# A scheduler's model learns the VectorE-GpSimd lock, and the low parts of the weights go to VectorE alone

## The chip, the cores and the metric

The kernel runs on one core of a Trainium2 chip. A core has a matrix engine (TensorE, PE in the profile, with PEld for the loading of its stationary operand), a vector engine (VectorE, DVE), an activation engine (ScalarE, ACT), a programmable engine (GpSimd, POOL) and a sync engine that here issues all DMAs (SyncE, SP). Each engine takes its own instructions strictly in order and waits on semaphores for the others. The metric is the device time of one execution in microseconds; lower is better.

## The reference

Two layers over 256 latent tokens and 256 context tokens of 1024 features. Layer 0 mixes tokens with a bidirectional RG-LRU, layer 1 with a bidirectional gated DeltaNet; each is followed by a SwiGLU feed-forward block (FFN), and each sub-layer is normalised and modulated by vectors that come from `c` and `c_ctx`. Cut to what matters:

```python
for layer in range(2):
    mod_l = split(silu(c) @ ada_w[layer] + ada_b[layer], 6)       # mod_c from c_ctx alike
    h = modulate(rmsnorm(x, norm_g[layer, 0]), mod_l[0], mod_l[1])
    if layer == 0:   # RG-LRU: u, y = split(h @ w_in); conv over 4 tokens; gates = sigmoid(u @ gate_w)
        a = exp(8 * r_gate * log_sigmoid(lam)); b = sqrt(1 - a * a) * (i_gate * u)
        y = (linear_scan(a, b) + reverse_scan(a, b)) * gelu(y) @ w_out
    else:            # gated DeltaNet: 8 key heads, 16 value heads of 128
        q, k, v = silu(conv(h @ w_in)); chunked: solve (I + strict(k k^T * decay)) u = rhs, state S
        y = (rmsnorm(o) * silu(z)) @ w_out
    x = x + mod_l[2] * y
    h = modulate(rmsnorm(x, norm_g[layer, 1]), mod_l[3], mod_l[4])
    x = x + mod_l[5] * ((silu(h @ w_gate) * (h @ w_up)) @ w_down)
return rmsnorm(x, final_norm_g)
```

## The kernel before

All products of weights run in a reduced-precision float32 format with both operands split in two parts: `hi` is the value rounded to that format, `lo = value - hi`. `mm3` adds three products (hi·hi, hi·lo, lo·hi). A weight tile of 128 x 1024 float32 comes by one DMA of 512 KB into `raw`; a copy with a change of type makes `whi`, and a subtraction makes `wlo` from `raw` and `whi`. Both happen in `weight()`, once for each of some 240 weight tiles; `split()` does the same for activations (`uh`/`ul`, `oh`/`ol`, `fh`/`fl`). So every weight tile costs one cast and one subtraction of 1024 columns on the element-wise engines before TensorE can use it.

The program is not written in the order in which it runs. A `Recorder` notes every instruction with its operands; at the end of a stage `flush()` gives them to a list scheduler. It keeps a clock for each engine, takes an estimate of each instruction's duration from `_cost()`, and places next the ready instruction with the lowest priority number (its place in the program plus a bias of its stage from the table `TUNE`). Some instructions have a choice of engine: `R.copy`, `R.scaled`, `R.plus` may go to ACT or DVE, `R.tt` (add, subtract or multiply of SBUF operands) to DVE or POOL; the scheduler takes the engine that by its estimates is done first. The order in the profile, L544 on every line, is what this left.

Before the change, `weight()` put `wlo` on DVE or POOL by `R.tt` in the stages marked wide (RG-LRU, both FFNs, output product) and in the z gates, and always on POOL in the rest of DeltaNet and for the weights that are made ahead of a stage (`aside=True`).

The stages in order of time, with the names that appear below:

- start: loads, norm, modulation of the first sub-layer (`ps_ada`)
- RG-LRU: products `ps_mm`, gate products `ps_g` from `uh`, `ul`; gates and scans (`th`, `nv`, `iu`, `a`) in 128 x 512 tiles on DVE; output `oh`, `ol`
- FFN of layer 0: gate and up products (`sg`, `fh`, `fl`), then down (`ps_dn`). Beside it the six modulation vectors of layer 1 are summed in the spare half of `x2` (the profile's `x<-ring,cs,x`, `x<-x,ring`)
- norm and modulation of layer 1 (`xg`, `hh`, `hl`, the last through `h` for half of the tiles)
- DeltaNet, in the order that `PROG` names by letters: A (products of a key head, convolution `cu` on DVE), E (decays `gn`, loaded by DMA from `rows`, masked by an affine select on POOL), N (systems of two key heads; elimination inside 32 x 32 blocks, one system to a lane: 30 steps of two dependent DVE instructions, `lmul<-lw` and `lw<-lw,lmul`), L (the blocks joined by small products on TensorE, `ps_w`, `ps_z`), P and C (attention weights `at`, queries `qg`, then the state over four chunks: `r`, `ps_y`, `S`, `kw`, `vb`), Z (z gates). There are four groups 0 to 3 of two key heads
- output product `ps_wo`, FFN of layer 1, final norm

Of the kernel before, what the change touches and what calls it, by code (L numbers as in the profile page):

```python
# [12 lines left out]
F32 = mybir.dt.float32  # L13
F32R = mybir.dt.float32r
AF = mybir.ActivationFunctionType
OP = mybir.AluOpType
# [10 lines left out]
# columns of the packed small-parameter array  # L27
# [10 lines left out]
# ---------------------------------------------------------------- program order  # L38
# The kernel is written down stage by stage; a list scheduler then orders the instructions of all
# engines, earlier stages first, so that later independent work fills an engine's waits. Tiles are  # L40
# allocated when their first instruction is placed.
def _shuffle(sh, pattern, sizes):
    """einops-like rearrange of a numpy array"""
# [33 lines left out]
class _Tile:  # L77
    def __init__(self, pool, shape, dtype, tag, bufs, name, dram):
# [7 lines left out]
        # a bank of PSUM is one region: its readers wait for all products into it  # L86
# [6 lines left out]
        self.group = [-1] * 4       # last product into the bank, per 32 partitions  # L93
        self.used = {}              # a bank serves one engine at a time: its last use by each
# [5 lines left out]
class _AP:  # L100
    """an access pattern of a tile that may not have its place yet"""
# [34 lines left out]
    def raw(self, offset, ap):  # L136
        """any pattern over a DRAM tile"""
        return self._with(("raw", offset, ap), self.sh)
# [25 lines left out]
class _Op:  # L164
    __slots__ = ("alts", "args", "kw", "tiles", "deps", "prio", "idx", "bytes", "succ", "ndep", "ready", "fin", "rows", "cols", "narrow")


_TABLE = {"Tanh": 7, "Exp": 1, "Gelu_apprx_tanh": 2, "Silu": 4, "Sqrt": 8}     # sets that hold the function
# [28 lines left out]
class Recorder:  # L197
    DMA_RATE = 360.0        # bytes / ns
    DMA_LATENCY = 2000
    TICK, TICK_COLUMNS = 10240 / 3, 3300  # L200
    # from the end of an instruction to the start of one that waits for it
# [15 lines left out]
    # ---- instructions with a choice of engine  # L217
# [22 lines left out]
    def tt(self, out, a, b, op):  # L240
        """add, subtract or mult of SBUF operands"""
# [3 lines left out]
    def mark(ap):  # L245
        """the instructions that have written ap so far, for after= of a later one"""
# [9 lines left out]
    # ---- costs in ns  # L256
    def _cost(self, eng, method, out, ins, kw, args):
        n = out.free() if isinstance(out, _AP) else 1
        src_psum = any(i.t.psum for i in ins) or (isinstance(out, _AP) and out.t.psum)
        if eng == "PE":  # L260
# [8 lines left out]
            if m <= 64:         # the column groups run side by side  # L269
# [3 lines left out]
        if eng == "DVE":  # L273
            if method == "transpose":
                return 1.04 * n + 70
# [12 lines left out]
        if eng == "POOL":  # L288
            if method == "dma_start":
                return 1000  # L290
            if method in ("memset", "affine_select"):
                return 0.6 * n + 60
            if kw.get("op", args[3] if len(args) > 3 else None) == OP.pow:
                return 165 * n + 298
            return 2.2 * n + 100
        return 60

# [255 lines left out]
def hybrid_block(ctx: ExitStack, tc: tile.TileContext, I, out, dbg=None):  # L553
# [1048 lines left out]
    X = {}  # L1602
# [117 lines left out]
```

## Time and profile before

| | us |
|---|---|
| three runs: median (lowest, highest) | 1481.32 (1480.1, 1487.81) |
| profiled execution: span from the first to the last instruction | 1474.6 |
| median less that span (what lies around it, and the spread of the runs) | 6.7 |
| busy in the profiled execution: PE / DVE / ACT / POOL | 1329.7 / 1149.3 / 552.4 / 430.8 |

The profiled execution has no time of its own beside its span. A busy time counts an instruction from its start to its end as the profile models it. PE's is no measure of its load, since matmuls overlap in the pipeline; its load is better read from the number of matmuls in a stretch. The last columns of a table by stretches are the granted TensorE clock (PEclk, 1.00 is full) and the DMA share. In a group of instructions the figures after the bar are busy us, mean ns of one, idle time of the engine before them, and what ended that idle time. A tile's view gives minimum, median and maximum in ns.

### The profile page before, as it was taken

To read this page: it belongs to the slowest core of one execution; us is meant where nothing else is said; L and a number is where in the kernel's file an instruction comes from. 1 tells how busy PE (TensorE), PEld (TensorE's weight loads), DVE (VectorE), ACT (ScalarE), POOL (GpSimd) and SP (SyncE) were. 2 spreads that over 40 slices of the span, in tenths; PEclk is the share of its full clock that TensorE was granted. 3 is DMA by queue.
4 is the path that set the end of the run, shared out by engine and by line. 5 is a ranking of instruction groups with operands and counts; after the bars stand their busy time and mean duration, and the time that the engine had idled before them with its cause. 6 is when DMAs were issued, how large, how long until landed. Compare 5 with 4: busy or idle time off the path is not lost.

```text
span 1474.6 us, 23548 instructions
## 1 busy us (share of the span) xinstructions
PE 1329.7 (90%) x9195; PEld 1135.7 (77%) x9195; DVE 1149.3 (78%) x1802; ACT 552.4 (37%) x1069; POOL 430.8 (29%) x357
## 2 busy tenths in 40 slices
PE   6998989999999999988767997888888898899997
PEld 3676758787778777886656786777788797899997
DVE  6899996778888885577689578699698767777765
ACT  3365562342323231025666434735634531211100
POOL 2134341111122111122545332643543521122111
PEclk9999999999999999999978789699599899999999
DMA  9544433355544564333842115315235205455563
GB/s 355 193 146 142 155 115 104 139 190 190 177 171 172 173 206 120 105 123 122 190 132 90 50 56 131 95 65 151 88 100 136 95 12 181 139 186 180 177 186 116
DMA packets 69790, 208.26 MB, mean 141 GB/s; under 512 B 6960, under 2 KB 14384, under 8 KB 69424
## 3 DMA queue, kind: packets, MB, share of 16 engines
q1 hardware_dynamic: 69680, 206.77, 44.1%
q8 instruction: 72, 1.18, 0.3%
q14 instruction: 38, 0.31, 0.1%
HBM read 196.71 MB, written 10.03 MB: 140 GB/s over the span
## 4 chain that ended last, share of the span: by engine, by line
PE 28%; DVE 17%; issue 3%; DMA 3%; POOL 1%; ACT 1%; POOLq 0%; SPq 0%; DVEq 0%; ACTq 0%
PE ps_mm L544 13%; DVE lw L544 4%; PE ps_dn L544 4%; DVE cu L544 3%; DVE lmul L544 2%; DMA qg<-rows 2%; PE ps_z L544 2%; PE ps_wo L544 2%; PE ps_w L544 2%; PE ps_y L544 2%; DVE whi L544 1%; PE ps_o L544 1%; DVE gn L544 1%; PE ps_g L544 1%; PE ps_s L544 1%
## 5 line engine op out<-in xcount | busy, mean ns | idle before, releaser
L544 PE MATMUL ps_mm<-hh,whi 128*128 128x512 f32 (+1 forms) x888 | 340.6, 385 | 35.3 <-DVE cu L544 18.2
L544 PE MATMUL ps_mm<-hh,wlo 128*128 128x512 f32 (+1 forms) x888 | 337.6, 381 | 18.1 <-POOL wlo L544 12.3
L544 PE MATMUL ps_mm<-hl,whi 128*128 128x512 f32 (+1 forms) x888 | 337.4, 381 | 0.3 <-DVE hl L544 0.3
L544 POOL TENSOR_TENSOR wlo<-raw,whi 128x1024 fp32r<-128x1024 f32 (+1 forms) x69 | 171.9, 2493 | 379.4 <-DVE whi L544 141.9
L544 DVE CAST whi<-raw 128x1024 fp32r<-128x1024 f32 (+1 forms) x185 | 139.3, 753 | 136.9 <-PE ps_mm L544 68.2
L544 PEld LDWEIGHTS ps_mm<-hh,whi 128*128 128x128 f32 x888 | 178.6, 202 | 73.6 <-issue 26.7
L544 DVE TENSOR_TENSOR wlo<-raw,whi 128x1024 fp32r<-128x1024 f32 (+1 forms) x169 | 214.7, 1271 | 11.3 <-ACT whi L544 1.4
L544 PEld LDWEIGHTS ps_mm<-hh,wlo 128*128 128x128 f32 x888 | 178.6, 201 | 50.0 <-POOL wlo L544 14.9
L544 PEld LDWEIGHTS ps_mm<-hl,whi 128*128 128x128 f32 x888 | 178.7, 201 | 29.0 <-issue 1.6
L544 PE MATMUL ps_dn<-fh,wlo 128*128 128x256 f32 (+1 forms) x374 | 122.5, 328 | 0.9 <-DVE wlo L544 0.9
L544 PE MATMUL ps_dn<-fh,whi 128*128 128x256 f32 (+1 forms) x374 | 122.9, 329 | 0.3 <-DVE whi L544 0.3
L544 PE MATMUL ps_dn<-fl,whi 128*128 128x256 f32 (+1 forms) x374 | 122.3, 327 | 0.0
L544 PE MATMUL ps_mm<-h2h,whi 128*128 128x256 f32 x352 | 100.1, 285 | 1.2 <-ACT h2h L544 1.2
L544 PE MATMUL ps_mm<-h2l,whi 128*128 128x256 f32 x352 | 100.5, 286 | 0.2
L544 PE MATMUL ps_mm<-h2h,wlo 128*128 128x256 f32 x352 | 100.1, 285 | 0.1
L544 POOL TENSOR_TENSOR x<-x,ring 128x1024 f32<-128x1024 f32 x13 | 37.0, 2850 | 166.3 <-ACT ring L544 166.3
L544 ACT ACTIVATE whi<-raw 128x1024 fp32r<-128x1024 f32 (+2 forms) x53 | 54.7, 1033 | 79.6 <-PE ps_mm L544 32.9
L544 ACT ACTIVATE fh<-sg 128x256 fp32r<-128x256 f32 (+1 forms) x43 | 22.4, 522 | 157.7 <-DVE sg L544 157.7
L544 PEld LDWEIGHTS ps_dn<-fh,wlo 128*128 128x128 f32 x374 | 71.1, 190 | 7.7 <-DVE wlo L544 1.8
L544 PEld LDWEIGHTS ps_dn<-fh,whi 128*128 128x128 f32 x374 | 71.1, 190 | 7.5 <-DVE whi L544 0.7
L544 ACT ACTIVATE ring<-ring,cs 128x1024 f32<-128x1024 f32 x42 | 48.3, 1150 | 74.3 <-DVE x L544 74.2
L544 PEld LDWEIGHTS ps_dn<-fl,whi 128*128 128x128 f32 x374 | 71.1, 190 | 5.9
(309 smaller groups left out, 2868.0 us busy)
## 6 DMA issues: line engine op xcount, KB each, us to landing
ring<-ada_w SPq DMA_DIRECT2D x96, 512.0 KB, 4.7
raw<-ffn_gu SPq DMA_DIRECT2D x88, 512.0 KB, 3.6
raw<-dn_w_in SPq DMA_DIRECT2D x49, 512.0 KB, 3.5
raw<-ffn_down SPq DMA_DIRECT2D x34, 512.0 KB, 3.6
raw<-rg_w_in SPq DMA_DIRECT2D x16, 512.0 KB, 3.8
gn<-rows SPq DMA_DIRECT2D x4, 2048.0 KB, 15.5
raw<-ffn_down SPq DMA_DIRECT2D x17, 384.0 KB, 3.4
raw<-dn_w_out SPq DMA_DIRECT2D x12, 512.0 KB, 3.5
```

Source lines behind the costliest of these rows:

```text
L544: call(*[real(x) for x in args], **{n: real(v) for n, v in kw.items()})
```

## The change

Three things change, and the rest of the diff removes comments.

1. The low parts. `weight()` and `split()` always subtract on DVE. No stage gives a low part to POOL any more.
2. The scheduler's estimates: a 32-block transpose on DVE costs 1.85 ns for a column where it cost 1.04; affine select and memset on POOL cost more, other POOL instructions 30 ns for the start where it was 100, and 2.25 ns for a column where it was 2.2; a DMA from `rows` that repeats its lines over partitions counts 2.3 times its bytes.
3. The lock. Each instruction has a class: DVE instructions with two SBUF inputs are class 1, copies and scalings from SBUF to SBUF class 2; POOL instructions are class 1, its memsets class 2. When one engine's last placed instruction still runs and the classes conflict, the scheduler lets the next one on the other engine start after it, or looks for another instruction or engine.

```diff
@@ _cost
             if method == "transpose":
-                return 1.04 * n + 70
+                return 1.85 * n + 70
@@ _cost, POOL
-            if method in ("memset", "affine_select"):
-                return 0.6 * n + 60
+            if method == "affine_select":
+                return 1.1 * n + 30
+            if method == "memset":
+                return 0.87 * n + 25
...
-            return 2.2 * n + 100
+            return 2.25 * n + 30
@@ new in Recorder
+    def _lock(eng, method, outs, ins):
+        if eng == "DVE":
+            wide = [x for x in ins if not x.t.psum and x.free() > 1]
+            if len(wide) > 1 or (len(wide) == 1 and method == "tensor_tensor" and len([x for x in ins if not x.t.psum]) > 1):
+                return 1
+            if method in ("tensor_copy", "tensor_scalar") and len(wide) == 1 and not outs[0].t.psum:
+                return 2
+            if method == "tensor_tensor" and len(ins) == 1 and wide:
+                return 1
+            return 0
+        if eng == "POOL":
+            return 2 if method == "memset" else 1 if method != "dma_start" else 0
+        return 0
@@ add_any
+            if any(o[0] == "raw" for y in ins for o in y.ops):
+                op.bytes *= 2.3
@@ flush, bank_free
-                return max((f + self.LATENCY[x][e] for t in op.tiles if t.psum for x, f in t.used.items() if x != e),
+                free = max((f + self.LATENCY[x][e] for t in op.tiles if t.psum for x, f in t.used.items() if x != e),
                            default=0.0)
+                mine, (until, theirs) = op.lock[e], held.get(e, (0.0, 0))
+                if mine and theirs:
+                    dve, pool = (mine, theirs) if e == "DVE" else (theirs, mine)
+                    if dve == 2 or pool == 1:
+                        free = max(free, until)
+                return free
...
+            if e in ("DVE", "POOL"):
+                held["POOL" if e == "DVE" else "DVE"] = (clock[e], op.lock[e])
@@ weight
-        (R.tt if (cur["wide"] or cur.get("flex")) and not aside else G.tensor_tensor)(lo[:, :cols], r[:, :cols], hi[:, :cols].bitcast(F32),
-                                                                 OP.subtract)
+        V.tensor_tensor(lo[:, :cols], r[:, :cols], hi[:, :cols].bitcast(F32), OP.subtract)
@@ split
-        R.tt(lo, src, hi.bitcast(F32), OP.subtract)
+        V.tensor_tensor(lo, src, hi.bitcast(F32), OP.subtract)
```

Counted over the whole program, DVE goes from 1804 to 1873 instructions, ACT from 1007 to 1060, POOL from 362 to 243; PE keeps 7530 and SP 429. POOL gives up 69 `wlo`, 22 `fl`, 9 `acc`, 5 `iu`, 5 `S`, 3 each of `qg` and `nv<-nv,y`, 2 each of `vb`, `ol1` and `wx`, and a few single ones; it takes 3 `hl` and keeps one more (14) of the sums `x<-x,ring`. Of the casts `whi`, 23 go from DVE to ACT, and so do 4 `a`, 3 `oh` and about 15 copies out of PSUM or between tiles in DeltaNet (`lw1`, `lw2`, `gn`, `zs`, `xo`). Between the first `u` and the first residual sum of the RG-LRU stage, DVE has 22 `wlo` where it had 10; between the first `cu` and the first output of `ps_wo` it has 57 where it had 16.

Three places show the order. First DVE in the RG-LRU stage, where two gate blocks are worked on (`whi` is a weight's cast, `th`, `nv`, `iu`, `a` are gate tiles). Before:

```order
L544 SCALAR_TENSOR_TENSOR th_995<-tr_989,th_995 128x512
L544 CAST whi_1040<-raw_902 128x1024
L544 SCALAR_TENSOR_TENSOR nv_1047<-th_995 128x512
L544 SCALAR_TENSOR_TENSOR iu_1036<-iu_1036,u_644 128x512
L544 SCALAR_TENSOR_TENSOR th_1049<-tr_1027,th_1049 128x512
L544 SCALAR_TENSOR_TENSOR iu_1068<-iu_1068,u_601 128x512
```

After:

```order
L576 CAST whi_1029<-raw_919 128x1024
L576 CAST uh_1035<-u_986 128x512
L576 SCALAR_TENSOR_TENSOR th_997<-tr_990,th_997 128x512
L576 TENSOR_TENSOR ul_1049<-u_986,uh_1035 128x512
L576 SCALAR_TENSOR_TENSOR nv_1056<-th_997 128x512
L576 SCALAR_TENSOR_TENSOR iu_1033<-iu_1033,u_644 128x512
L576 SCALAR_TENSOR_TENSOR th_1044<-tr_1026,th_1044 128x512
L576 TENSOR_TENSOR wlo_1075<-raw_919,whi_1029 128x1024
```

The low part of the weight that was cast stood on POOL before; now it stands on DVE, seven instructions behind its cast.

Second, DVE inside the elimination of group 0 in DeltaNet. Before:

```order
L544 TENSOR_TENSOR lw_5777<-lw_5777,lmul_5827 128x21x10
L544 CAST whi_5938<-raw_5791 128x1024
L544 TENSOR_SCALAR cu_5947<-ps_mm_5789,sm_82 128x512
L544 TENSOR_TENSOR lmul_5827<-lw_5777 128x220
L544 SCALAR_TENSOR_TENSOR cu_5947<-ps_mm_5789,sm_82,cu_5947 128x2x254
L544 TENSOR_TENSOR lw_5777<-lw_5777,lmul_5827 128x20x11
```

After:

```order
L576 TENSOR_TENSOR lmul_5863<-lw_5777 128x210
L576 TENSOR_TENSOR wlo_6009<-raw_5615,whi_5951 128x1024
L576 TENSOR_TENSOR lw_5777<-lw_5777,lmul_5863 128x21x10
L576 TENSOR_TENSOR wlo_6023<-raw_5878,whi_5990 128x1024
L576 TENSOR_TENSOR lmul_5863<-lw_5777 128x220
L576 TENSOR_TENSOR at_5788<-ps_kq_5771,at_5788 128x512
```

Low parts now stand between two steps of the elimination; the convolution `cu` stood there before.

Third, PE where stage L of the last group begins (`ps_w1` and `ps_z` are its small products, `ps_mm` the z gates). Before:

```order
L544 MATMUL ps_w1_9767<-ldt_9744,gn_8315 32x32 x32
L544 MATMUL ps_w1_9808<-ldt_9744,gn_8315 32x32 x32
L544 MATMUL ps_mm_9847<-hh_4912,whi_9735 128x256
L544 MATMUL ps_mm_9847<-hl_4923,whi_9735 128x256
L544 MATMUL ps_mm_9847<-hh_4912,wlo_9790 128x256
```

After:

```order
L576 MATMUL ps_wo_9835<-zero_8590 128x512
L576 MATMUL ps_wo_9828<-oh1_9842,whi_9785 128x256
L576 MATMUL ps_w1_9868<-ldt_9856,gn_8461 32x32 x32
L576 MATMUL ps_w1_9912<-ldt_9856,gn_8461 32x32 x32
L576 MATMUL ps_z_9953<-ld_9848,lw1_9919 32x32 x2
```

The products of the z gates are no longer between the small products. Over the four L stages, 127 large `ps_mm` products stood between the small ones before and 13 do now; the others have moved ahead, 480 instead of 411 of them before the first L stage.

More of the change, by code (lines that the diff above doesn't have):

```diff
@@ L164 @@
 class _Op:
-    __slots__ = ("alts", "args", "kw", "tiles", "deps", "prio", "idx", "bytes", "succ", "ndep", "ready", "fin", "rows", "cols", "narrow")
+    __slots__ = ("alts", "args", "kw", "tiles", "deps", "prio", "idx", "bytes", "succ", "ndep", "ready", "fin", "rows", "cols", "narrow",
+                 "lock")
 _TABLE = {"Tanh": 7, "Exp": 1, "Gelu_apprx_tanh": 2, "Silu": 4, "Sqrt": 8}
@@ L290, in _cost @@
                 return 1000
-            if method in ("memset", "affine_select"):
-                return 0.6 * n + 60
+            if method == "affine_select":
+                return 1.1 * n + 30
+            if method == "memset":
+                return 0.87 * n + 25
             if kw.get("op", args[3] if len(args) > 3 else None) == OP.pow:
                 return 165 * n + 298
-            return 2.2 * n + 100
+            return 2.25 * n + 30
         return 60
+    @staticmethod
+    def _lock(eng, method, outs, ins):
[11 more added lines that the diff above has]
+        return 0
     def add(self, eng, method, fn, a, k):
@@ L313, in add_any @@
         op.args, op.kw = a, k
-        op.alts = {}
+        op.alts, op.lock = {}, {}
         for eng, m, fn, a2, k2 in alts:
@@ L320, in add_any @@
             op.alts[eng] = (self._cost(eng, m, out, ins, k2, a2), table, fn, a2, k2)
+            op.lock[eng] = self._lock(eng, m, outs, ins)
         op.bytes = 0
@@ L427, in flush @@
                 offer(op)
-        dma_free, table, done = 0.0, 1, 0
+        dma_free, table, done, held = 0.0, 1, 0, {}
         at_tick, columns, slow, rows, narrow = 0, 0.0, False, 1, False
```

## The prediction

> **What bounds the kernel now.** I read the table by stretches first, then the groups of instructions, then single instructions in time. Columns: busy us (and instructions) of PE, PEld, DVE, ACT, POOL; PEclk; DMA share; GB/s.
>
> ```profile
> span 1474.6 us, 23548 instructions
> 54.00:220.00 166.00, 155.20 (x761) 110.38 (x760) 158.10 (x203) 97.65 (x133) 58.21 (x35) 0.97 0.44 146
> 281.00:544.00 263.00, 257.32 (x1199) 204.11 (x1200) 215.50 (x206) 79.63 (x97) 42.79 (x15) 1.00 0.53 182
> 570.00:630.00 60.00, 60.00 (x278) 48.97 (x277) 29.81 (x38) 3.20 (x8) 9.61 (x4) 1.00 0.34 99
> 675.00:748.00 73.00, 51.64 (x254) 42.19 (x253) 48.46 (x95) 42.02 (x98) 35.99 (x34) 0.86 0.64 167
> 748.00:815.00 67.00, 52.69 (x231) 42.68 (x232) 64.30 (x119) 42.82 (x101) 37.33 (x24) 0.85 0.31 99
> 815.00:861.00 46.00, 42.51 (x556) 37.00 (x555) 25.25 (x38) 17.57 (x31) 11.92 (x9) 0.70 0.11 36
> 1279.00:1408.00 129.00, 129.00 (x1075) 129.00 (x1076) 91.30 (x113) 17.28 (x43) 26.49 (x22) 1.00 0.56 182
> ```
>
> In RG-LRU (54 to 220) DVE is idle for 7.9 us of 166: DVE bounds it. In the FFNs (281, 570, 1279) PE has no gap worth the name and DVE has 38 us or more to spare in the long ones. DeltaNet (675 to 1238) alternates: in the elimination (748) DVE is idle for 2.7 us of 67, in stage L (815) for 21 of 46, while PE goes through small products at a granted clock of 0.70.
>
> What does POOL's work cost DVE? A step of the elimination, the step before it, and the low part that POOL ran:
>
> ```profile
> 759.77 0.33 DVE L544 TENSOR_TENSOR lmul<-lw 128x168 f32<-128x168 f32 x1
> 760.99 2.47 DVE L544 TENSOR_TENSOR lmul<-lw 128x184 f32<-128x184 f32 x1
> 760.84 2.40 POOL L544 TENSOR_TENSOR wlo<-raw,whi 128x1024 fp32r<-128x1024 f32 x1 [1.60 <-DVE whi L544]
> ```
>
> The second step starts 0.15 us after POOL's and ends 0.22 us behind it (763.46 against 763.24): it took 2.47 us for work of about 0.35. It was held, so this low part cost DVE 2.1 us. On DVE itself, where nothing disturbs (in the FFN of layer 1), a low part and a cast take:
>
> ```profile
> L544 DVE TENSOR_TENSOR wlo<-raw,whi 128x1024 fp32r<-128x1024 f32 x36 | 44.0, 1222 | 2.2 <-DVE whi L544 0.5
> L544 DVE CAST whi<-raw 128x1024 fp32r<-128x1024 f32 x37 | 25.7, 695 | 28.9 <-PE ps_mm L544 28.9
> ```
>
> So a low part on POOL costs DVE between nothing (DVE happens to work from PSUM or waits) and about 2.1 us, on DVE always 1.22. The exchange pays where POOL holds DVE up more than 58% of the time.
>
> **RG-LRU, 54 to 220.** The groups of DVE in that stretch, the range of one of them, the modulation products on PE, and what PE waited for a low part (us, times, longest; 60 to 330):
>
> ```profile
> L544 DVE SCALAR_TENSOR_TENSOR iu<-iu,u 128x512 f32<-128x512 f32 x16 | 19.7, 1233 | 0.0
> L544 DVE TENSOR_TENSOR_SCAN nv<-a,iu 128x512 f32<-128x512 f32 x8 | 15.8, 2003 | 0.0
> L544 DVE SCALAR_TENSOR_TENSOR nv<-th 128x512 f32<-128x512 f32 x16 | 13.2, 823 | 0.1
> L544 DVE TENSOR_TENSOR iu<-nv,iu 128x512 f32<-128x512 f32 x10 | 13.1, 1337 | 0.1
> L544 DVE TENSOR_TENSOR_SCAN nv<-a,iu 128x256 f32<-128x256 f32 x8 | 5.1, 662 | 0.0
> L544 DVE SCALAR_TENSOR_TENSOR iu<-iu,u x16: 678/686/2905, 73.3 to 196.1; 128x512 f32<-128x512 f32 x16
> L544 PE MATMUL ps_ada<-ring,cs 128*32 128x256 f32 x192 | 15.3, 391 | 0.0
> PE ps_mm L544 <- POOL wlo L544: 5.1, 3, 2.7
> ```
>
> An undisturbed 512-column instruction takes 0.686 us (the median), a scan of 512 columns 2 x 0.662 = 1.324. The excess: 16 x (1.233 - 0.686) = 8.8; 16 x (0.823 - 0.686) = 2.2; 10 x (1.337 - 0.686) = 6.5; 8 x (2.003 - 1.324) = 5.4. Together 22.9 us in four groups alone. After the change POOL has one 512-column product there, so nearly all of this goes. Added on DVE: 12 low parts, 12 x 1.222 = 14.7; nine or ten products and sums that POOL had, 9.5 x 0.686 = 6.5; less one cast (0.7) and seven copies of 512 columns, each at most 0.686 (4 at the middle). Net +16.5. DVE gains at least 22.9 - 16.5 = 6.4 us.
>
> The other end is PE's need: 761 - 192 = 569 large products at 60/278 = 0.216 us (the row from 570), 123 us, and 48 sets of four modulation products side by side at 0.391, 19 us: 142 of 166. No more than 24 us can go. Smaller groups of DVE are stretched too, and PE's waits for POOL's low parts (5.1 us up to 330) go as well, so I take a value between: **-12** (ends -6 and -20).
>
> **Norms, 220 to 281 and 649 to 675.** Here sums and lifts lie on the path to the first product of the next stage, and POOL made low parts ahead of it:
>
> ```profile
> L544 DVE TENSOR_TENSOR acc<-acc,sq x34: 408/424/2200, 6.4 to 1243.9; 128x256 f32<-128x256 f32 x29, 128x512 f32<-128x512 f32 x5
> L544 DVE TENSOR_TENSOR hl<-h,hh 128x256 fp32r<-128x256 f32 x8 | 3.4, 429 | 0.1
> L544 DVE SCALAR_TENSOR_TENSOR hl<-xg,mod,hh 128x256 fp32r<-128x256 f32 x8 | 5.9, 737 | 0.0
> L544 DVE TENSOR_SCALAR hh<-xg,mod 128x256 fp32r<-128x256 f32 x5 | 3.8, 769 | 0.1
> L544 DVE TENSOR_SCALAR h<-xg,mod 128x256 f32<-128x256 f32 x2 | 0.7, 346 | 0.0
> ```
>
> One sum took 2.2 us for 0.42, 1.8 held; the second `hl` row costs 0.31 us more for each than the first, 8 x 0.31 = 2.5; `hh` costs 0.42 more than `h`, which has the same shape, 5 x 0.42 = 2.1. Held: 6.4. Five low parts come to DVE in the two stretches, 6.1, of which I leave 2.4 on the path, two of the five, since DVE waits for PE and norms in the rest. **-4** (ends 0, if all five lie on the path, and -6.4).
>
> **DeltaNet, 675 to 1238.** The elimination of the four groups on DVE (the two instructions of each step, then the sum over the four stretches), and the low parts on POOL in the same stretches:
>
> ```profile
> 748.00:815.00 67.00, 35.06 (x60) 0.85 0.31 99
> 861.00:911.00 50.00, 23.74 (x59) 0.97 0.35 103
> sum 233.00, DVE 110.21; mean DVE 27.55
> 748.00:815.00 67.00, 21.53 (x10) 0.85 0.31 99
> 861.00:911.00 50.00, 5.67 (x3) 0.97 0.35 103
> 969.00:1022.00 53.00, 9.48 (x4) 0.97 0.38 116
> 1079.00:1142.00 63.00, 9.85 (x4) 0.92 0.42 113
> ```
>
> The same 60 instructions take 35.06 us beside ten low parts and 23.74 beside three: (35.06 - 23.74) / 7 = 1.62 us for each. 21 low parts there: 34 us. The 19 others of this stage fall on transposes, work from PSUM and waits; I give them a fifth of that price, 6. Held in all: 40. Added on DVE: 41 x 1.222 = 50, and some eight products and sums of `S`, `vb`, `qg`, `ol1` (about 4); removed: 8 casts (5.6) and about 15 copies of some 0.5 us that go to ACT (7.5). Net +41. So DVE's load does not fall: 41 - 40 = +1, between -14 (if the other work of POOL no longer holds it either) and +15 (if the 1.62 is half due to that other work).
>
> One rule speaks against this trade. The Trainium skill's page "Perfetto Trace Analysis", section "Optimizing Scalar/DVE Operations", says that where DVE is saturated, giving work to ScalarE or even GpSimd may make sense, though between DVE and GpSimd it might not help, since they share a read port. If handing over were free, taking it back would add the whole +41; by the rows of the elimination it adds +1. The 2.47 us step sides with the page's reservation.
>
> What can still shorten the stage is the order. PE waited there for:
>
> ```profile
> PE ps_mm L544 <- DVE cu L544: 18.2, 7, 6.2
> PE ps_mm L544 <- POOL wlo L544: 7.2, 4, 4.8
> 724.87 2.34 POOL L544 TENSOR_TENSOR wlo<-raw,whi 128x1024 fp32r<-128x1024 f32 x1
> L544 DVE STREAM_TRANSPOSE lw<-gn x16: 1894/1976/2047, 747.6 to 1085.2; 32x1024 f32<-32x1024 f32 x16
> ```
>
> The waits for `wlo` can halve, -4; the low part at 724.87 stands between the masks of `gn` that the first elimination needs, -2; a scheduler that knows of 40 us of holding and of transposes at 1.98 us instead of 1.13 (1.04 x 1024 + 70 ns) plans the evacuation of `cu` later and ACT's share larger, so a tenth of the 18.2, -2. In sum **-7** (ends +15 and -30; -30 if every such wait goes and the load falls by 14).
>
> **The rest.** The FFNs are at nothing: in layer 1, 22 `fl` of 256 columns come to DVE, 22 x 0.42 = 9 us (the median of `acc`, of the same shape), covered by its 38 idle us (129 - 91.3); if that cover went they would cost 9. In layer 0 PE bounds, and POOL keeps the sums of the modulation, 14 of them. Loads are issued in the same order on SP, so the waits for `rows` stay.
>
> Sum: -12 - 4 - 7 = -23; span 1474.6 - 23 = 1451.6. The median of the runs lies 6.7 above the profiled span, so 1458.3: **1458 us**, with a range of its own from 1440 to 1473.
>
> **The rivals.**
>
> *DeltaNet becomes longer.* POOL's work was free where DVE did something else, and now it is not: the low parts now stand in the elimination, which every group's L stage waits for, and L has lost its cover: 114 large products (127 less 13) at 0.12 us (129/1075) to 0.216 us, 14 to 25 us, have moved to where DVE is already full. For it: DVE idle for 2.7 us of 67. Against: PE's clock of 0.70 in L means that it has time there now, and the products must run somewhere in any case. If none of them finds a gap, +25, and with the load at its upper end +15: 1481.3 - 16 + 40 = 1505. It decides from +24 in DeltaNet on.
>
> *The gains cancel.* RG-LRU saves 6, the norms nothing, DeltaNet loses its upper 15 in part: 1481 - 6 + 8 = 1483. The same comes out if the holding was not what stretched those instructions; against that stand start and end of the 2.47 us step.
>
> *The new order is worth more.* DVE's idle time in L (21 us of 46) and PE's waits shrink together, DeltaNet -30: 1481 - 16 - 30 = 1435. For it: the scheduler had the 16 transposes above, and eight more like them, at little over half their length. Against: DVE's load stays.
>
> **How the numbers follow.** Forecast (1440 to 1473) 0.58; the order worth more (1420 to 1440) 0.16; cancelled (1474 to 1488) 0.15; DeltaNet longer (about 1505) 0.11. Faster by over 0.5% (below 1474, about what a measurement of this kernel tells from no change) 0.74, same 0.15, slower 0.11. The range of 8 in 10 leaves out the last case and the lower half of the second: 1430 to 1487.
>
> **What would show it.** Right: RG-LRU shorter by 6 to 20 us with `iu<-iu,u` near 0.69 us; every elimination near 19 us for its 60 instructions; no 2.2 us `acc`; POOL without `wlo`. Wrong: DVE's gaps between the eliminations longer than before, or PE waiting for `wlo` on DVE in DeltaNet for more than the 7.2 us that it waited for POOL.

## The result and the profile after

The changed kernel takes 1431.5 us (median of four runs, 1427.4 to 1436.1) against 1480.7 (four runs, 1475.6 to 1487.8) on the same chip: a ratio of 0.9667, 95% interval 0.9621 to 0.9714. That is 49 us less, where 23 were forecast, and 8.5 us below the lower end of the forecast's range. The profiled execution has a span of 1425.3 us and a time of 1427.4, so what lies around the span is 2.1 us; the rest of the 6.7 that I took for it was the spread of the runs. Span against span the gain is 49.3.

From the page, the span and the busy times:

```profile
span 1425.3 us, 23473 instructions
...
PE 1316.9 (92%) x9195; PEld 1132.9 (79%) x9195; DVE 1092.9 (77%) x1871; ACT 590.5 (41%) x1122; POOL 189.5 (13%) x238
```

The table by stretches, columns as in the prediction. First two stretches of before that were not shown (gate and up products of layer 0, DeltaNet), then after: RG-LRU, gate and up, DeltaNet, the first L stage.

```profile
281.50:544.00 262.50, 257.25 (x1199) 204.04 (x1200) 215.06 (x205) 79.22 (x96) 42.79 (x15) 1.00 0.53 183
674.50:1238.00 563.50, 473.64 (x4182) 422.00 (x4183) 444.33 (x876) 280.12 (x650) 244.80 (x228) 0.85 0.37 104
```

```profile
53.00:210.00 157.00, 150.88 (x759) 109.79 (x758) 139.09 (x215) 105.98 (x145) 3.59 (x13) 0.98 0.46 155
267.50:522.00 254.50, 254.50 (x1200) 204.58 (x1199) 190.42 (x195) 91.45 (x108) 35.30 (x13) 1.00 0.57 189
645.60:1190.40 544.80, 472.65 (x4184) 422.24 (x4185) 432.77 (x909) 293.00 (x668) 137.44 (x177) 0.85 0.36 108
787.50:823.00 35.50, 33.51 (x534) 30.54 (x533) 19.64 (x34) 17.97 (x35) 5.82 (x9) 0.76 0.17 58
```

Measured from marks that both kernels have (the first `u`, the first residual sum, the first `sg`, and so on), the 49 us come from these places:

| stage | before | after | difference | forecast |
|---|---|---|---|---|
| start | 54.1 | 52.7 | -1.4 | 0 |
| RG-LRU | 166.2 | 157.3 | -8.9 | -12 |
| norm after it | 61.1 | 57.3 | -3.8 | -4 with the next norm |
| gate and up, layer 0 | 262.5 | 254.5 | -8.0 | 0 |
| down products | 105.5 | 104.5 | -1.0 | 0 |
| norm, layer 1 | 25.1 | 19.4 | -5.7 | (see above) |
| DeltaNet | 563.6 | 544.8 | -18.8 | -7 |
| the rest | 236.5 | 235.0 | -1.5 | 0 |

Three stages carry what was missed: DeltaNet with 12 us, gate and up with 8, the norms with 5.5.

The groups that were stretched before are whole now. In RG-LRU a view of the tile `iu`, then two groups, the first of them the low parts, 22 on DVE where it had 10:

```profile
L576 DVE SCALAR_TENSOR_TENSOR iu<-iu,u x16: 683/685/692, 71.5 to 182.8; 128x512 f32<-128x512 f32 x16
```

```profile
L576 DVE TENSOR_TENSOR wlo<-raw,whi 128x1024 fp32r<-128x1024 f32 x22 | 26.8, 1217 | 1.3 <-ACT whi L576 1.0
...
L576 DVE SCALAR_TENSOR_TENSOR nv<-th 128x512 f32<-128x512 f32 x16 | 10.9, 684 | 0.0
```

`iu` went from a mean of 1.233 us to 0.685, `nv` from 0.823 to 0.684. The 60 instructions of each elimination, which took 35.06, 23.74 and so on, in all 110.21:

```profile
712.00:788.00 76.00, 21.36 (x60) 0.88 0.37 122
823.00:894.00 71.00, 20.79 (x60) 0.98 0.51 138
937.00:991.00 54.00, 20.18 (x60) 0.97 0.38 100
1038.00:1105.00 67.00, 19.70 (x60) 0.95 0.41 130
```

That is 82.0 in all, 28 less. What PE waits for in DeltaNet is of another kind (us, times, longest):

```profile
PE ps_kq L576 <- DVE gn L576: 11.2, 2, 11.0
PE ps_w L576 <- DVE ldt L576: 10.4, 3, 5.0
PE ps_mm L576 <- DVE wlo L576: 6.1, 8, 2.6
PE ps_mm L576 <- DVE cu L576: 3.0, 6, 1.0
```

The wait for `cu`, 18.2 before, is 3.0; the wait for a low part is about as long as it was, on DVE now. POOL's waits for the repeated rows, before and then after:

```profile
POOL at L544 <- DMA qg<-rows: 24.6, 6, 10.1
POOL gn L544 <- DMA gn<-rows: 20.5, 4, 7.3
```

```profile
POOL gn L576 <- DMA gn<-rows: 12.8, 4, 6.8
POOL at L576 <- DMA qg<-rows: 12.0, 7, 5.1
```

### The profile page after: what moved, and what is told of

It is laid out like the page before. It is cut to its first block, busy times and chain, and to the rows that moved or that the text cites. A ratio compares the mean times of both kernels' runs of the same rounds, so it can differ in the third digit from the quotient of the medians.

```text
span 1425.3 us, 23473 instructions
## 1 busy us (share of the span) xinstructions
PE 1316.9 (92%) x9195; PEld 1132.9 (79%) x9195; DVE 1092.9 (77%) x1871; ACT 590.5 (41%) x1122; POOL 189.5 (13%) x238
## 5 line engine op out<-in xcount | busy, mean ns | idle before, releaser
L576 PE MATMUL ps_mm<-hh,whi 128*128 128x512 f32 (+1 forms) x888 | 330.5, 374 | 14.4 <-ACT whi L576 5.9
L576 PE MATMUL ps_mm<-hh,wlo 128*128 128x512 f32 (+1 forms) x888 | 326.5, 370 | 12.3 <-DVE wlo L576 12.2
L576 PE MATMUL ps_mm<-hl,whi 128*128 128x512 f32 (+1 forms) x888 | 328.3, 371 | 0.2 <-DVE hl L576 0.2
L576 DVE TENSOR_TENSOR wlo<-raw,whi 128x1024 fp32r<-128x1024 f32 (+1 forms) x238 | 293.8, 1235 | 30.7 <-ACT whi L576 22.4
L576 DVE CAST whi<-raw 128x1024 fp32r<-128x1024 f32 (+1 forms) x162 | 111.5, 688 | 137.1 <-PE ps_mm L576 72.5
L576 PEld LDWEIGHTS ps_mm<-hh,whi 128*128 128x128 f32 x888 | 171.4, 194 | 50.9 <-issue 11.2
L576 PEld LDWEIGHTS ps_mm<-hh,wlo 128*128 128x128 f32 x888 | 171.3, 193 | 44.0 <-DVE wlo L576 17.7
L576 PEld LDWEIGHTS ps_mm<-hl,whi 128*128 128x128 f32 x888 | 171.8, 194 | 27.0 <-issue 1.2
L576 ACT ACTIVATE whi<-raw 128x1024 fp32r<-128x1024 f32 (+2 forms) x76 | 78.1, 1029 | 102.1 <-PE ps_mm L576 58.9
L576 PEld LDWEIGHTS ps_mm<-h2h,whi 128*128 128x128 f32 x352 | 68.3, 194 | 1.8 <-ACT h2h L576 1.8
```

Source lines behind the costliest of these rows:

```text
L576: call(*[real(x) for x in args], **{n: real(v) for n, v in kw.items()})
```

## The experiments

The change has three parts that can be had apart: the move of the low parts, the lock rule, and the estimates (transposes, POOL, repeated rows). Times are medians; each set of runs has its own runs of the kernel before, medians 1478 to 1485, and its ratio is to these. Stage lengths come from the one profiled execution of each kernel, which lies up to 7 us from the kernel's median (14 in e6), so a few us of a stage tell nothing.

### The parts

Theory A was that of the prediction: the move gives back time in which DVE was held. Rival B: the scheduler's model makes a better order, whoever subtracts. e1 is the kernel before with the low parts on DVE; e2 adds the lock rule, e3 the estimates; e4 is the changed kernel with the low parts by the old rule.

The diff of e1 is against the kernel before, those of e2 to e4 against the changed one (in e2 POOL's old costs and the bare bytes come back in the same way, in e1 and e4 the line of `split()` changes too):

```diff
@@ e1
-        (R.tt if (cur["wide"] or cur.get("flex")) and not aside else G.tensor_tensor)(lo[:, :cols], r[:, :cols],
+        V.tensor_tensor(lo[:, :cols], r[:, :cols],
@@ e2
-                return 1.85 * n + 70
+                return 1.04 * n + 70
@@ e3
-                if mine and theirs:
+                if False:
@@ e4
-        V.tensor_tensor(lo[:, :cols], r[:, :cols],
+        (R.tt if (cur["wide"] or cur.get("flex")) and not aside else G.tensor_tensor)(lo[:, :cols], r[:, :cols],
```

> Every low part on DVE, but the scheduler's estimates and rules as before the change (no lock, old durations). Theory A (holding: POOL's low parts held DVE, and taking them away is what gains): most of the 49 us, -30 to -40 against before, about 1445; the rest of 10 to 15 us is the lock rule's, since the sums of the modulation would still collide with casts and low parts in the FFN of layer 0 (about 25 us of DVE held there, 8 us of its length). Rival B (order: DVE's load hardly changes, and the gain is that the scheduler plans with true numbers): within 10 us of before, about 1475.

> Low parts on DVE and the lock rule, with the old durations. Theory A: all but a few us of the change, about 1435, and the FFN of layer 0 as short as after the change. Rival B with the durations as the cause: about 1465, the gain of 49 less than half there.

> Low parts on DVE and the new durations, no lock rule. Theory A: about 1440 to 1445, the FFN of layer 0 some 5 to 8 us longer than after the change. Rival B with the durations as the cause: about 1432, as after the change.

> Lock rule and new durations, but low parts on DVE or POOL by the old rule (POOL always, in most of DeltaNet and for weights made ahead). Theory A: -10 to -20, about 1463: in RG-LRU and the FFNs the scheduler can flee POOL, in DeltaNet the 40 low parts still go there and hold DVE. Rival B: -35 or more, 1445 or below.

To complete the table, e5 has the estimates alone and e9 the lock rule alone: e5 is e4 without the rule, e9 is e4 with the old estimates.

```diff
@@ e5, against e4
-                if mine and theirs:
+                if False:
@@ e9, against e4
-                return 1.85 * n + 70
+                return 1.04 * n + 70
```

> Only the estimates of durations are new; low parts go to GpSimd by the old rule and the scheduler has no lock rule. Theory D (true durations carry DeltaNet, whoever makes the low parts): DeltaNet 535 to 545 us of its 564, the stages ahead of it as before (RG-LRU 162 to 166, gate and up 262), total near 1461. Rival M (in DeltaNet the durations help only beside the move or the lock rule, since each run that gained there had one of them): DeltaNet 555 to 566, total 1475 to 1485.

> The kernel before with the lock rule alone: low parts by the old choice, old estimates. So far the estimates alone gave nothing (1490), the move alone -20, move and estimates -48, lock rule and estimates -50. Theory S (the plan is good once the held time is either gone by the move or known by the lock rule, and the estimates pay only on top of one of the two): the lock rule alone does what the move alone did, 1460 to 1470, and DeltaNet stays at 555 to 590. Rival R (the lock rule is the main thing and the estimates matter only beside the move): 1430 to 1445, DeltaNet 535 to 550. Rival N (it is worth nothing without the estimates): 1476 to 1490.

Measured, with start to the first `cu` and DeltaNet from the profile:

| run | move | lock rule | estimates | median us | ratio, interval | to `cu` | DeltaNet |
|---|---|---|---|---|---|---|---|
| before | | | | 1481 to 1485 | 1 | 674.6 | 563.6 |
| e5 | | | x | 1490.6 | 1.0044 (1.0019, 1.0069) | 672.3 | 580.7 |
| e9 | | x | | 1470.0 | 0.9919 (0.9890, 0.9947) | 654.5 | 582.0 |
| e1 | x | | | 1464.2 | 0.9862 (0.9824, 0.9899) | 657.2 | 563.8 |
| e2 | x | x | | 1464.5 | 0.9867 (0.9838, 0.9897) | 642.9 | 587.4 |
| e3 | x | | x | 1436.1 | 0.9685 (0.9640, 0.9729) | 655.7 | 537.4 |
| e4 | | x | x | 1433.2 | 0.9654 (0.9627, 0.9680) | 659.2 | 535.0 |
| after | x | x | x | 1431.5 | 0.9667 (0.9621, 0.9714) | 645.6 | 544.8 |

Theory A fell as an account of the whole: the move alone gives 20 us, where A had 30 to 40 and B at most 10, and the kernel with 49 low parts still on POOL (e4) is as fast as the changed one, as B had it. What stands: ahead of DeltaNet the move gives 17 us (657.2) and the lock rule gives 10 to 20, with or without it. These two are not independent. Where the old rule leaves the choice to the scheduler, the lock rule makes it take DVE of itself: in e9 POOL has 2 low parts in the RG-LRU stage, where it had 12, and 47 in the whole program, where it had 69.

Three stage times ahead of DeltaNet, which are used below (us):

| | before | e1, move | e9, lock rule | e2, both | after |
|---|---|---|---|---|---|
| RG-LRU | 166.2 | 161.4 | 162.4 | 157.2 | 157.3 |
| RG-LRU and both norms | 252.4 | 237.2 | 242.2 | 233.9 | 234.0 |
| gate and up, layer 0 | 262.5 | 262.2 | 255.4 | 254.5 | 254.5 |

In DeltaNet the move alone gives nothing (563.8), the lock rule alone costs 18 and beside the move 24, and the estimates bring 26 to 47, but only beside one of the other two; alone they cost 17. So theory S, written for e9, came out, at the edge of its range: in these kernels better estimates gain only where the held time is gone or known. Whoever makes the low parts, a planner that has the estimates, and either knows the lock or has few held instructions to know of, ends within 5 us of the same time.

### Which estimate

First each alone, on the kernel before (e7 takes the masks' new costs too).

```diff
@@ e6
-                return 1.04 * n + 70
+                return 1.85 * n + 70
@@ e7
-            return 2.2 * n + 100
+            return 2.25 * n + 30
@@ e8
+            if any(o[0] == "raw" for y in ins for o in y.ops):
+                op.bytes *= 2.3
```

> The kernel before with one new estimate: the 32-block transposes at 1.85 ns a column (they take 1.98 us, the scheduler believed 1.13). Theory D1 (the sixteen transposes around the eliminations and the eight more like them, each believed 0.83 us too short, put the plan of DVE in DeltaNet off by some 20 us, and that is what the estimates mend): DeltaNet 540 to 548, total 1461 to 1468. Rival D2 (it is the DMAs of repeated rows, or POOL's masks, which decide when a group's systems are ready): DeltaNet 558 to 566, total 1477 to 1485.

> The kernel before with new estimates for POOL alone (affine select and memset dearer, the start of other instructions 30 ns for 100). Theory D1 (transposes carry it): DeltaNet within 5 us of 564, total 1476 to 1488. Rival D2 (the masks): DeltaNet 540 to 550, total 1462 to 1470.

> The kernel before with one new estimate: a DMA that repeats rows counts 2.3 times its bytes. Theory D1 (transposes carry it): DeltaNet within 5 us of 564, total 1476 to 1488. Rival D2 (the loads of the decays, believed done too early, put masks and eliminations in the plan ahead of what can run): DeltaNet 540 to 550, total 1462 to 1470.

e6: 1481.1 (ratio 0.9996, 0.9962 to 1.0029); e7: 1502.7 (1.0159, 1.0083 to 1.0234), slower by 0.8 to 2.3%; e8: 1479.0 (0.9964, 0.9937 to 0.9991). No estimate alone does anything worth having, as e5 has it for the three: e6 denies D1, e7 and e8 deny D2. (The profiled execution of e6 was 14 us faster than its median; its stages are not used.) They had to be asked beside the other parts: the changed kernel with one estimate put back at a time.

```diff
@@ e10
-                return 1.85 * n + 70
+                return 1.04 * n + 70
@@ e11
-            return 2.25 * n + 30
+            return 2.2 * n + 100
@@ e12
-                op.bytes *= 2.3
+                op.bytes *= 1.0
```

> The changed kernel with one estimate put back: transposes at 1.04 ns a column. The order differs from DeltaNet on only. Beside move and lock rule the three estimates together are worth 33 us. If the transposes carry them: DeltaNet 565 to 587, total 1450 to 1465. If POOL's costs or the repeated rows do: DeltaNet within 6 us of 545, total 1426 to 1438.

> The changed kernel with POOL's old estimates (0.6 ns a column for masks, 100 ns for the start of the rest). If POOL's costs carry the 33 us: DeltaNet 565 to 587, total 1450 to 1465. If the transposes or the repeated rows do: DeltaNet within 6 us of 545, total 1426 to 1438; the stages ahead may shift by 2 us either way, since the whole order is planned anew.

> The changed kernel with the repeated rows counted at their bare bytes again. If they carry the 33 us (the plan has the decays in place too early and keeps DVE and POOL for masks and systems that cannot start): DeltaNet 565 to 587, total 1450 to 1465. If transposes or POOL's costs do: DeltaNet within 6 us of 545, total 1426 to 1438.

e10: 1425.6 (0.9619, 0.9572 to 0.9666); e11: 1433.2 (0.9680, 0.9634 to 0.9726); e12: 1455.6 (0.9826, 0.9784 to 0.9868). So beside the other parts the estimate of the repeated rows carries 24 us of the 33 that the three are worth (e2 against the changed kernel); those of the transposes and of POOL, each put back alone, carry nothing that is measured, and the other 9 us were not traced.

What does the planner learn from it? The loads of `rows` in the changed kernel, from 676 to 720 us (KB each, median us to landing), and the DMA share and GB/s of the first 36 us, of a stretch in which nearly only rows move, and of one in which weights and spills move among them:

```profile
gn<-rows SPq DMA_DIRECT2D x2, 2048.0 KB, 20.5
raw<-dn_w_in SPq DMA_DIRECT2D x3, 512.0 KB, 17.0
qg<-rows SPq DMA_DIRECT2D x2, 512.0 KB, 30.2
kspill<-k SPq DMA_DIRECT2D x1, 256.0 KB, 18.6
```

```profile
0.00:36.00 36.00, 22.86 (x130) 13.16 (x130) 21.21 (x59) 12.24 (x28) 3.35 (x20) 1.00 0.94 354
678.00:690.00 12.00, 12.00 (x80) 10.70 (x79) 10.87 (x19) 8.04 (x20) 2.17 (x2) 1.00 0.69 195
690.00:705.00 15.00, 10.49 (x47) 8.32 (x45) 7.64 (x12) 10.71 (x31) 8.53 (x13) 0.92 0.93 200
```

The DMA engines move 195 to 200 GB/s there, where they moved 354 at the start, though from 690 us on they are as busy as there (0.93 and 0.94). The planner reckons 360 GB/s (`DMA_RATE`), so by these rows the true factor is about 1.8; the change has 2.3. All that stands behind in the queue is late: a weight of 512 KB lands after 17.0 us (3.6 to 4.7, by the medians of the whole program), the spill of `k` after 18.6 us. With bare bytes the planner believes these done and puts next what waits for them. So it is in e12, where DVE does nothing for 14.8 us in front of a tile whose buffer the spill of `k` still reads, and PE behind it:

```profile
714.54 0.61 DVE L576 TENSOR_SCALAR vp<-ps_vt,nkh 128x128 f32<-128x128 f32 x2 [14.81 <-DMA kspill<-k]
```

```profile
PE ps_ssq L576 <- DVE vp L576: 17.4, 1, 17.4
```

e2, which has the bare bytes too, waits 16.7 us at the same place for the same spill.

In the changed kernel the same spill is as late, and DVE works: from 705 to 720 us it is busy for 14.74 us, in e12 for 4.96.

```profile
705.00:720.00 15.00, 5.54 (x20) 4.27 (x20) 14.74 (x20) 11.03 (x25) 8.80 (x14) 0.50 0.66 190
```

```profile
705.00:720.00 15.00, 2.87 (x9) 2.52 (x10) 4.96 (x11) 2.27 (x3) 7.76 (x10) 0.50 0.61 186
```

### Is it that wait?

e13 takes this wait away in e12, e14 in the changed kernel, by a third buffer (for `vp` and `zs`, which share it, as well; the squares make room).

```diff
-        k = dn.tile([128, 4, 128], F32, tag="kv", bufs=2, name="k")
+        k = dn.tile([128, 4, 128], F32, tag="kv", bufs=3, name="k")
-        sq = dn.tile([128, 256], F32, tag="sqq", bufs=1, name="sqq")
+        sq = tmp(256, name="sqq")
```

> The kernel with the repeated rows at their bare bytes (1455.6), and a third buffer for the tiles `k` and `vp` (two shared before; the squares `sqq` and `junk` move to the temporaries to make room). There DVE stands 14.8 us before `vp`, in front of a full queue, until the spill of `k`, which lies behind 3 MB of rows, has landed. Theory W (that wait is what the estimate of the rows avoids): the gap goes, DeltaNet falls by 12 to 20 us to 556 to 564, total 1435 to 1444. Rival V (the estimate works over all four groups through the masks and weights on POOL, the gap in the first is made up later): 1450 to 1458.

> The changed kernel with the same third buffer. Theory W: its plan has gone round that wait already (its spill lands 18.6 us after the issue, and DVE works meanwhile), so at most 3 us either way: 1427 to 1435. Rival V: the buffer is worth something of its own, 1415 to 1426.

e13: 1457.7 (0.9798, 0.9723 to 0.9873), e14: 1423.3 (0.9585, 0.9527 to 0.9642). The wait in front of `vp` went from 14.8 us to 2.3 in e13, and the stretch from the first `cu` to the first transpose of group 0 is 10 us shorter (81.4 to 71.4); yet DeltaNet takes 578.0 as against 576.2. So theory W fell, and both runs lie where rival V had them. That the buffer is worth something of its own in the changed kernel is not shown by e14: its interval overlaps that of the changed kernel. In e13 the time came back at other waits of the same kind:

```profile
898.72 1.23 POOL L576 TENSOR_SCALAR_AFFINE_SELECT at<-qg 128x512 f32<-128x512 f32 x2 [11.57 <-DMA qg<-rows]
899.92 1.01 POOL L576 TENSOR_TENSOR fo<-sso,nhalf 128x4 f32<-128x4 f32 x1
```

```profile
DVE oa L576 <- POOL fo L576: 17.3, 3, 9.4
```

POOL stands 11.57 us before a mask of `qg`, whose rows have not landed; `fo`, a power of 4 columns, is next in its queue; DVE waits for `fo`, 17.3 us in three times (8.9 in e12, and no such wait in the changed kernel).

Is it the lateness of `qg` or that of `gn` that must be known? e17 gives only the `qg` loads their 2.3, e18 (`> 1024` in the same place) only the `gn` loads.

```diff
-            if any(o[0] == "raw" for y in ins for o in y.ops):
+            if any(o[0] == "raw" for y in ins for o in y.ops) and x.free() <= 1024:
```

> The changed kernel, where only the loads `qg` of repeated rows (512 KB) count 2.3 times their bytes; `gn` (2 MB) counts its bare bytes. Theory Q (with the old bytes the planner believes `qg` in place, puts its masks `at` on POOL early, and POOL stands there up to 25 us with `fo` and others behind it, for which DVE and PE wait): it is enough that `qg` is known late, POOL's wait for `qg` falls from 62 us to 10 to 25, DeltaNet 540 to 555, total 1422 to 1436. Rival G (the 2 MB of `gn` ahead of all in the queue is what must be known): DeltaNet 565 to 580, total 1447 to 1460.

> The reverse: `gn` counts 2.3 times its bytes, `qg` its bare bytes. Theory Q, with `qg` behind `gn` in the queue: the planner now knows 8 of the some 10 us by which `qg` is late, so most of the gain comes here too: 1428 to 1442, POOL's wait for `qg` 20 to 40 us. Rival G: all of it, as the changed kernel, 1424 to 1432. If neither load alone is enough: 1447 to 1460 here and in the other run.

e17: 1437.2 (0.9729, 0.9688 to 0.9770), e18: 1434.7 (0.9702, 0.9675 to 0.9730): either load alone gives most of the gain, 18 and 21 of the 24 us by medians, 14 and 18 by the ratios. Theory Q had e18 so, and e17 comes out 1 us above its range; rival G fell with e17. The mark that I had set for theory Q, POOL's wait for `qg`, was a bad one. In e17 it is 16.6 us, as expected. In e18:

```profile
POOL at L576 <- DMA qg<-rows: 68.3, 6, 28.0
```

```profile
DVE oa L576 <- POOL fo L576: 1.6, 1, 1.6
```

POOL waits longer than in e12 (62.0), and the kernel is 21 us faster than e12: DVE's wait for `fo`, behind it, is 1.6 us. Taking together DVE's waits for `vp` and for `fo`, on the spill or on POOL: e12 23.7 us, e13 19.4, e17 10.9, e18 2.0, after none; DeltaNet takes 576, 578, 549, 554, 545. The two go together over the five, roughly. They do not elsewhere: e5 has 2.2 us of such waits and takes 580.7. So these waits are part of what the rows cost, and that they are all of it was not shown.

### A better version

Since e4 was better in DeltaNet and the changed kernel ahead of it, e15 has the low parts on POOL again in DeltaNet outside the z gates, and e16 leaves them there to the scheduler's choice.

```diff
@@ e15
-        V.tensor_tensor(lo[:, :cols], r[:, :cols],
+        (V if cur["wide"] or cur.get("flex") else G).tensor_tensor(lo[:, :cols], r[:, :cols],
@@ e16
-        V.tensor_tensor(lo[:, :cols], r[:, :cols],
+        (V.tensor_tensor if cur["wide"] else R.tt)(lo[:, :cols], r[:, :cols],
```

> The changed kernel, but in DeltaNet outside the z gates the low parts go to GpSimd again, as before. Ahead of DeltaNet it is the changed kernel (646 us to the first `cu`), in DeltaNet close to the kernel that had the model alone (535 us there, 49 low parts on GpSimd). If stages add: 1425 - 10 = 1415 to 1423. If holding in DeltaNet costs as much as the exchange saves: 1428 to 1434.

> The changed kernel, but in DeltaNet each low part goes to the engine that the scheduler takes, with the lock rule and the measured durations. If the plan's choice is better than either rule: 1412 to 1422. If it is no better than always DVE: 1427 to 1435.

e15: 1419.7 (0.9562, 0.9505 to 0.9619), DeltaNet 540.6 with 30 low parts on POOL; e16: 1425.8 (0.9602, 0.9546 to 0.9658). e15 has the lowest median of the study; e14 (1423.3) cannot be told from it. Its interval ends just below where that of the changed kernel begins (0.9621, on another chip), so the lead over it, about 1%, is likely and not more. The stages added up nearly as expected (644.5 us to the first `cu`, and 540.6 where 535 was hoped for). e16 lies between its two ranges: the scheduler, too, leaves 30 low parts on POOL there, and DeltaNet takes 544.1, as in the changed kernel.

## Why the prediction was right or wrong

The direction was right, and so was the mechanism of holding; the size was half of what came. 1431.5 lies below the forecast's range of 1440 to 1473, just inside the wider one of 8 in 10, and among the times of the rival "the new order is worth more".

The step that failed is the price of the scheduler's model. The prediction gave it -2 in half a sentence, for transposes and holding, and gave the estimate of the rows nothing ("the waits for `rows` stay"). The runs showed in its place that the model carries more than half of the gain: the move alone gives 20 us (e1), the model without the move as much as the whole change (e4), and in the changed kernel the estimate of the rows is worth 24 us in DeltaNet (e12) and the lock rule 8 in gate and up (262.2 in e1, 254.5 in e2).

The forecast was, nearly, one of the move alone, and that is in part luck. Up to the first `cu` e1 gives -17.4 where the terms of RG-LRU and the norms say -16; but RG-LRU gave less than its term and the norms more, and in DeltaNet, where the forecast says -7, e1 gives 0.

**RG-LRU, -12 forecast, -8.9 measured.** Inside its ends; the held time came back as worked out, and the bound was misread. DVE's busy time fell by 19.0 (158.10 to 139.09), far more than the 6.4 that were certain, and the stage by less than half of it. So "DVE bounds it" holds only in part: PE is busy for 150.9 of 157 us now (155.2 of 166 before); what bounds the stage now no run shows. The 161.4 us of e1 cannot be set against the 157.3: in e1 PE runs 28 more products within this stretch (10 of `ps_mm`, 18 of `ps_ada`), which otherwise stand in the norm behind it, about 4 us by the prediction's prices of a product. RG-LRU and the norms together can be compared: -15.2 by the move alone, -18.4 by the whole change.

**Norms, -4 forecast, -9.5 measured.** Right in kind, too small. The held rows came back as worked out: `hl` from 737 ns to 476, `hh` from 769 to 360.

```profile
L576 DVE SCALAR_TENSOR_TENSOR hl<-xg,mod,hh 128x256 fp32r<-128x256 f32 x8 | 3.8, 476 | 0.0
L576 DVE TENSOR_SCALAR hh<-xg,mod 128x256 fp32r<-128x256 f32 x3 | 1.1, 360 | 0.0
```

The mis-sized terms are the 2.4 us of low parts that I left on the path, and that only DVE's time was counted: the stages shortened by more than the 6.4 us held. In e1 the two norms give -10.4, of which some 4 are the products that RG-LRU took over.

**FFNs at nothing.** Right for layer 1 (129.0 us before and after), wrong by 8 us for gate and up of layer 0. "In layer 0 PE bounds" is the step that failed, and "no gap worth the name" before it: the row that I showed leaves PE idle for 5.7 us of 263, and 1199 matmuls take 262.5 us before, 1200 take 254.5 after. Most of that idle time was spent waiting for low parts on DVE (in the changed kernel 0.6 us is left):

```profile
PE ps_mm L544 <- DVE wlo L544: 4.6, 6, 1.8
```

What held DVE was to be read in the casts there. The groups of before, of e1 (262.2 us) and of the changed kernel:

```profile
L544 DVE CAST whi<-raw 128x1024 fp32r<-128x1024 f32 x40 | 38.6, 965 | 16.4 <-PE ps_mm L544 16.4
```

```profile
L574 DVE CAST whi<-raw 128x1024 fp32r<-128x1024 f32 x39 | 40.1, 1028 | 14.9 <-PE ps_mm L574 14.9
```

```profile
L576 DVE CAST whi<-raw 128x1024 fp32r<-128x1024 f32 x28 | 19.4, 692 | 25.1 <-PE ps_mm L576 25.1
```

A cast takes 0.692 us when nothing holds it; beside POOL's sums `x<-x,ring` the mean was 0.965, 11 us of holding in a stage whose low parts were nearly all on DVE already. I had seen that POOL keeps these sums, and had asked only what the moved instructions cost. The move does nothing for it (e1); the lock rule does (254.5 in e2 as well, and 255.4 in e9, with the lock rule alone): it keeps the casts clear of the sums and gives 12 of them to ACT. Which of the two is worth how much was not separated.

**DeltaNet, -7 forecast, -18.8 measured.** By DVE's books the failed term is the load, +1. The low parts added 49 us (50 forecast), the eliminations gave back 28 (34), casts 5.7 (5.6), the copies some 8 (7.5); but the other held work gave back 19 to 24 us where I allowed 6, "a fifth of that price". Group by group, at like counts, it is 19.3 us in the changed kernel and 11.5 in e1. So POOL's low parts held twice what I allowed outside the eliminations, and the rest came with the lock rule and the estimates. One such group, before and after:

```profile
L544 DVE TENSOR_TENSOR zs<-zs,onl 128x512 f32<-128x512 f32 x6 | 6.9, 1154 | 0.8 <-ACT zs L544 0.8
```

```profile
L576 DVE TENSOR_TENSOR zs<-zs,onl 128x512 f32<-128x512 f32 x6 | 4.1, 684 | 0.0
```

So DVE's busy time fell by 11.6 us (444.33 to 432.77), and its idle time by 7.1, about the -8 forecast for the order. But that 8 is right by accident. The experiments show large terms of opposite sign in it. The lock rule beside the old estimates takes DVE's idle time in DeltaNet from 123.7 us (e1) to 151.4 (e2): it is the rival "DeltaNet becomes longer", with +24, by another mechanism than the one that I gave. The row estimate takes it back, from 137.0 (e12) to 112.0 (after). The reason that I gave, a planner that knows of transposes of 1.98 us, is worth nothing (e10, 1425.6). And the sentence "Loads are issued in the same order on SP, so the waits for `rows` stay" failed: POOL's waits for rows went from 45.1 us to 24.8, since an estimate need not move a load to change what is put behind it. The diff showed the factor 2.3; I did not cost it. Two slips in the sum decide nothing: 41 low parts less 21 are 20, not 19, and the end -30 is less than its own condition gives (18.2 + 7.2 + 14 = 39).

**The rivals.** "The new order is worth more" gave 1435, close to the time, on the ground of the 16 transposes; the time was right and the ground was not. The rule of the Trainium skill that was weighed, in "Perfetto Trace Analysis", section "Optimizing Scalar/DVE Operations", that handing work from DVE to GpSimd might not help, is borne out ahead of DeltaNet, where taking it back gave 17 us; in DeltaNet the traces go the other way: with the lock and the rows in the plan, handing over 30 to 35 low parts is as good or a little better (e4 535.0, e15 540.6, after 544.8).

**What would show it.** `iu` near 0.69 (0.685), POOL without `wlo`, eliminations near 19 (19.7 to 21.4), PE's wait for `wlo` on DVE under 7.2 (6.1) and no longer gaps (DVE idle for 15.9 us in the first L stage, 21 before) came so. One sum `acc` of 2.4 us is left, beside the one sum of the modulation that POOL keeps in the down products.

**What stays open.** Why the true estimates cost 6 us as long as neither move nor lock rule is there, and gain 28 to 37 as soon as one is. It fits that a plan which is wrong by the held time loses what better numbers give, but no run shows this by itself. Nor is it shown that the rows gain because their price is true: of factors only 1 and 2.3 were run, and the traces say about 1.8. And each kernel is one order of many; e7 shows that one small change of an estimate can cost 20 us, so a difference between two single runs may in part be an accident of the order. For the estimates as a whole that is unlikely, since three pairs agree (e1 and e3, e9 and e4, e2 and the changed kernel).

## What to carry to other kernels

When a change touches a planner's model, price the model as a part of its own, term by term: here it was worth more than the instructions that it moved, and its parts did not add (the estimates alone +6 us, beside either of the others -28 or -37). Ask of every estimate which queue it speaks of, and list what stands in order behind the late thing, on the DMA queue and on the engine that waits for it; that wait's length says little (62 us in e12, 68 in e18, which is 21 us faster), and what is due behind it says more. And before a stage is put at nothing because its engine is the bound, compare the mean of each group on the feeding engine with the same group where nothing disturbs it.

## What the hardware showed that I had not expected

A cast with one SBUF input is held by POOL as well, not only an instruction with two. In e1 a cast of 128 x 512, otherwise 0.43 us, started 0.68 us after a sum on POOL and ended 0.28 us behind it:

```profile
310.51 2.00 DVE L574 CAST fh<-sg 128x512 fp32r<-128x512 f32 x1
323.88 0.43 DVE L574 CAST fh<-sg 128x512 fp32r<-128x512 f32 x1
```

```profile
309.83 2.40 POOL L574 TENSOR_TENSOR x<-x,ring 128x1024 f32<-128x1024 f32 x1 [9.31 <-ACT ring L574]
```

The Trainium skill has this in "SBUF — State Buffer", section "SBUF: two separate sides": VectorE's two-port modes lock out GpSimd, and are locked out by it, like its operations with two SBUF inputs. The trace agrees for the cast, which is locked out here; that a cast locks out POOL is not among the lines shown.

And loads that repeat a row over partitions move 195 GB/s at a DMA share of 0.69 when nearly alone, and 200 at 0.93 with weights and spills among them, where the first 36 us move 354 at 0.94: about 1.8 times the time for a byte. In the queue they made a 512 KB weight land after 17.0 us.
